# A list schedule's cost table in a hybrid decoder block: new estimates for scans, matmuls, transposes and GpSimd operations

## The chip, the core and the metric

The kernel runs on one core of a Trainium2 chip, as one launch. The metric is the device time of that launch in microseconds (us). The profile names the engines PE (TensorE matmul), PEld (TensorE's weight loads), DVE (VectorE), ACT (ScalarE), POOL (GpSimd) and SP (SyncE, which issues most DMAs). Each engine works off its own instructions in the order in which the program issued them, and waits on semaphores for the others.

## The reference, cut to what matters

```python
xn   = rms_norm(x, norm1_g)                         # x: 1024 tokens x 1024
proj = xn @ w_in                                    # to 44 blocks of 128 columns
q_sb, k_sb, v_sb, q_hg, f_hg, i_hg, g_hg, gate_sb, gate_hg = split_cols(proj, IN_SIZES)
# 8 stick-breaking heads of 64: z = q.k/8 under the strict causal mask
#   w = exp(log_sigmoid(z) - sum of softplus(z) over the keys between), o = w @ v
o_sb = stick_breaking_attention(rms_norm(q), rms_norm(k), v)
# 4 gated recurrent heads of 128: S_t = diag(f_t) S_{t-1} + (1-f_t) i_t^T, o_t = S_t^T q_t
o_hg = hgrn2_mixer(q_hg, f_hg, i_hg, g_hg, lb, hg_norm_g)
mixed = sigmoid(gate_sb) * (o_sb @ w_branch[:512]) + sigmoid(gate_hg) * (o_hg @ w_branch[512:])
h = x + mixed @ w_out
out = h + (silu(hn @ w_gate) * (hn @ w_up)) @ w_down     # hn = rms_norm(h, norm2_g)
```

All data are float32. The sums over keys in the attention and over time in the recurrent heads are running sums, which VectorE computes with its scan instruction.

## The kernel before, in words

Activations are kept transposed, channels on the 128 partitions and tokens along the free axis, in two halves of 512 tokens. A float32 product is made of three matmuls: both operands are split into a high part (rounded to the type fp32r, which the matmul takes) and a low part (the rest), and high x high, high x low and low x high are added in PSUM.

The kernel has stages one behind the other. **Stage 1**, the only one that the change touches, holds the first norm, the input projection, the attention heads and the recurrent heads. Behind it come the branch product (lines 774 to 810), the output product, the gated FFN and the down product, whose order is written out in the program and stays as it is.

Stage 1 is not issued in the order in which it is written down. `Plan` (lines 74 to 197) records every instruction as an operation with an engine, an **estimated duration** in us, a rank, the operations that must come before it and the buffers it uses. `Plan.issue` then runs a list scheduler: it steps a clock, keeps for each engine the time at which it is free, and at each step gives a free engine the first operation in its list that is ready and whose buffers are to be had. The list is sorted by rank, then by `way`, the longest chain of estimated durations from the operation to the end. What it issues is the real instruction; what stays of the plan is only the **order** on each engine. A result travels for a fixed estimated time (`FROM` and `TO`: 0.14 us, 0.2 us out of TensorE, 0.35 us into it, 2.0 us out of a DMA).

The estimates come from small helpers:

- `A` (line 360) for ScalarE and `V` (line 364) for VectorE: a constant and the number of elements per partition at 1200 or 960 per us.
- `G` (line 368) for GpSimd: a number given at each call.
- `M` (line 371) for a group of matmuls: columns by 2400 per us and 0.003 us for each matmul; `T` (line 377) for transposes; `L` (line 382) for loads on SP's queue: 350 KB per us, at least 0.47 us.

On them stand the parts that the prediction speaks of:

- `take_x` (line 441) loads x, splits it, and adds up the eight squared tiles, some on GpSimd, some on VectorE; `M(2048 * 2, ...)` in line 468 sums them over the channels, and `rstd` makes the norm's factor. Nothing that leaves a projection can go on before that factor.
- `proj` (line 474) issues one projected block of 128 channels and 512 tokens as 8 operations of 3 matmuls into one of three PSUM banks `pj`. Its rank is -1, so it is **filler**: TensorE takes it when nothing else is ready. The blocks come in one fixed order (`fill`, from the strings in line 30). A block for head pair u+1 has to wait until head pair u has released its buffers (`gate`, line 760); the 16 blocks "G" (the output gates) have no such wait. The last five blocks are "G".
- `split_w` (line 430) splits half a weight tile: the high part on GpSimd (`pool_copy`), the low part `ol` on VectorE.
- `scores` (line 548): six copies by DMA gather one attention head (`qs`, `ks`), then for each block of queries the matmuls `z` (two PSUM banks), on ScalarE the steps to softplus, on VectorE one add (`aa<-z,aa`), the **scan** (line 580) and the difference `ww<-z,aa` (line 584), which is the last reader of the bank `z`.
- `values` (line 589): transposes of the weights (`ms<-ident,ww`), the split into `th` and `tl`, and the product with v.
- `hgrn` (line 637): four scans of 128 tokens (line 649), seven levels of decayed products (line 657, `ms<-ql,dl`), the state update, and the sums by `sums` (line 489), whose high part is made on GpSimd.

Of the kernel before, what the change touches and what calls it, by code (L numbers as in the profile page):

```python
# [15 lines left out]
ALU = mybir.AluOpType  # L16
# [3 lines left out]
P = 128  # L20
# [180 lines left out]
def hybrid_block(ctx: ExitStack, tc, xT, wi, wb, wo, wg, wu, wd, vec, outT):  # L201
    nc = tc.nc
# [44 lines left out]
    ident = const1.tile([P, P], F32, name="ident")  # L247
# [10 lines left out]
    ones = const1.tile([P, P], F32, name="ones")  # L258
# [32 lines left out]
    def hs(h):  # L291
        return slice(h * HALF, (h + 1) * HALF)
# [42 lines left out]
    plan = Plan()  # L335
# [16 lines left out]
    def new(tag, shape=(P, HALF), dt=F32):  # L352
        pool, cap = where[tag]
        plan.ring(tag, cap)
        return Buf(tag, lambda: pool.tile(list(shape), dt, tag=tag, bufs=cap, name=tag))
# [6 lines left out]
        return plan.op("A", us, [(fn, args, kw)], rank, part=part, holds=holds)  # L362

    def V(fn, *args, n=HALF, aps=0, rank=0, part=False, holds=(), **kw):
        us = 0.07 + n / 960 + 0.061 * aps
        return plan.op("V", us, [(fn, args, kw)], rank, part=part, holds=holds)

    def G(fn, *args, us, rank=0, after=(), holds=(), **kw):
        return plan.op("G", us, [(fn, args, kw)], rank, after, holds=holds)

    def M(cols, mms, rank=0, after=(), holds=()):

        return plan.op("P", cols / 2400 + 0.003 * len(mms),
                       [(nc.tensor.matmul, m[:3], dict(start=m[3], stop=m[4])) for m in mms],
                       rank, after, holds=holds)

    def T(outs, after=(), holds=()):

        return plan.op("P", 0.11 * len(outs), [(nc.tensor.transpose, (o, i, ident), {})
                                               for o, i in outs], 0, after, holds=holds)  # L380

    def L(dst, src, kb, rank=0, after=(), part=False):
# [15 lines left out]
        A(act, a, a, AF.Exp)  # L398

    def pool_copy(dst, src, rank=0, after=(), holds=()):  # L400
        return G(nc.gpsimd.tensor_scalar, dst, src, 1.0, 0.0, op0=ALU.mult, op1=ALU.add, us=0.6,
                 rank=rank, after=after, holds=holds)

    lvl_mask = []
# [20 lines left out]
    last_load, last_split = [None], [None]  # L425

    def load(dst, src, kb):
        last_load[0] = L(dst, src, kb, rank=1, after=(last_load[0],))
# [12 lines left out]
    def take_x(h):  # L441
        ss, acc, ws, sqs = new("ms"), new("tail"), [[], []], []
        for k in range(KT):
            x = new("aa" if h == 0 else ("xf", "xq", "xi", "xg")[k // 2])
            load(x, xT[k][:, hs(h)], 256)
            if h == 0 and k in (0, 1, 3, 4):
                u, i = k % 3, k // 3
                n, v = fill[u]
                w = new("kb")
                load(w, wi[COL[n] + v][:, hs(i)], 256)  # L450
                ws[u].append(split_w(w))
            g = vt[:, V_N1 + k:V_N1 + k + 1]
            A(act, xh[k][h][:, hs(h)], x, AF.Copy, scale=g, aps=1, rank=2 - h)
            V(stt, xl[k][h][:, hs(h)], x, g, xh[k][h][:, hs(h)].bitcast(F32), op0=ALU.mult,
              op1=ALU.subtract, aps=1, rank=2 - h)
            if k == 0:
                A(act, acc, x, AF.Square, rank=1 - h)
            else:
                sq = new("ww")
                A(act, sq, x, AF.Square, rank=1 - h)  # L460
                sqs.append(sq)
        nv = 3 + h
        for sq in sqs[:7 - nv]:
            G(nc.gpsimd.tensor_tensor, acc, acc, sq, op=ALU.add, us=1.15, after=(last_split[0],))
        for sq in sqs[8 - nv:]:
            V(tt, sqs[7 - nv], sqs[7 - nv], sq, op=ALU.add, rank=1 - h)
        V(tt, acc, acc, sqs[7 - nv], op=ALU.add, rank=1 - h)
        M(2048 * 2, [(ss, ones, acc, True, True)])
        rstd(rr[h], ss, D, rank=1 - h)
        return ws  # L470

# [17 lines left out]
    def sums(out, src, w, n, after=()):  # L489

        hi, lo = new("th", dt=F32R)[:, :n], new("tl", dt=F32R)[:, :n]
        G(nc.gpsimd.tensor_scalar, hi, src, 1.0, 0.0, op0=ALU.mult, op1=ALU.add,
          us=0.05 + n / 930, holds=(lo,) if after else (lo, out))
        V(tt, lo, src, hi.bitcast(F32), op=ALU.subtract, n=n)
        return M(2 * n, [(out, w, hi, True, False), (out, w, lo, False, True)], after=after)

# [140 lines left out]
    def hgrn(hd, last):  # L637
        d = heads[hd]
        lbs, oml, nom = lb[:, hd:hd + 1], omlb[:, hd:hd + 1], nomlb[:, hd:hd + 1]
        state = None  # L640
        cs = [slice(c * P, (c + 1) * P) for c in range(4)]
        chunk = lambda t: t.rearrange("p (c t) -> p c t", t=P)
        for h in range(2):
            sf, q, vtok = d["hf", h], d["hq", h], d["hi", h]
            lf, key, bb, at = new("tmp"), new("kb"), new("kb"), new("kb")
            A(act, lf, sf, AF.Ln, bias=lbs, scale=oml, aps=2, holds=(key, bb, at))
            d["free hf", h] = V(ts, key, sf, nom, oml, op0=ALU.mult, op1=ALU.add, n=256, aps=2)
            for c in cs:
                V(nc.vector.tensor_tensor_scan, bb[:, c], lf[:, c], lf[:, c], 0.0, op0=ALU.add,
                  op1=ALU.min, n=P)  # L650
            pair = lambda t, m: t.rearrange("p (n u m) -> p n u m", u=2, m=m)
            G(nc.gpsimd.tensor_tensor, at, key, q, op=ALU.mult, us=1.15, after=(last,))
            dg = new("ms")
            last = sums(dg, at, ones_r, HALF, (last,))
            V(tt, chunk(at), chunk(dg),
              ident.rearrange("p (o t) -> p o t", o=1).to_broadcast([P, 4, P]), op=ALU.mult)
            for li, m in enumerate(LEVELS):
                nb = HALF // (2 * m)
                bv = pair(bb, m)
                if m == 1:  # L660
                    e1 = new("ql", (P, HALF // 2))
                    ev = e1.rearrange("p (n m) -> p n m", m=1)
                    V(tt, ev, bv[:, :, 1, :], bv[:, :, 0, :], op=ALU.subtract, n=256)
                    A(act, e1, e1, AF.Exp, n=256)
                    for t, u in ((key, 0), (q, 1)):
                        G(nc.gpsimd.tensor_tensor, ev, ev, pair(t, 1)[:, :, u, :], op=ALU.mult,
                          us=0.6)
                    lv = new("ms")
                    last = sums(lv[:, :256], e1, ones_r, 256, (last,))
                    V(nc.vector.copy_predicated, pair(at, 1)[:, :, 1, :],  # L670
                      lvl_mask[li - 1].rearrange("p c (n m) -> p (c n) m", m=1),
                      lv[:, :256].rearrange("p (n m) -> p n m", m=1), n=256)
                    continue
                rb = bv[:, :, 0, m - 1:m].to_broadcast([P, nb, m])
                dl, ql = new("dl"), new("ql", (P, HALF // 2))
                dv = pair(dl, m)
                V(tt, dv[:, :, 0, :], rb, bv[:, :, 0, :], op=ALU.subtract, n=256)
                V(tt, dv[:, :, 1, :], bv[:, :, 1, :], rb, op=ALU.subtract, n=256, part=True)
                A(act, dl, dl, AF.Exp)
                V(tt, ql.rearrange("p (n m) -> p n m", m=m), pair(q, m)[:, :, 1, :], dv[:, :, 1, :],  # L680
                  op=ALU.mult, n=256)
                V(tt, dv[:, :, 0, :], dv[:, :, 0, :], pair(key, m)[:, :, 0, :], op=ALU.mult, n=256)
                lv = new("ms")
                n = P - m
                last = M(8 * (n + 64), [(lv[:n, c * 64:(c + 1) * 64], dl[:, c * P:c * P + n],
                                         ql[:, c * 64:(c + 1) * 64], True, True)
                                        for c in range(4)], after=(last,))
                dst, src = pair(at, m)[:n, :, 1, :], lv[:n, :256].rearrange("p (n m) -> p n m", m=m)
                if m == 64:
                    V(nc.vector.tensor_copy, dst, src, n=256)  # L690
                else:
                    V(nc.vector.copy_predicated, dst,
                      lvl_mask[li - 1][:n].rearrange("p c (n m) -> p (c n) m", m=m), src, n=256)
            kd, ktok, qe, bl = new("tail"), new("tail"), new("tail"), new("bl", (P, 4))
            b3 = chunk(bb)
            V(tt, chunk(kd), b3[:, :, P - 1:P].to_broadcast([P, 4, P]), b3, op=ALU.subtract,
              holds=(ktok, qe, bl))
# [6 lines left out]
            d["free hq", h] = V(tt, qe, qe, q, op=ALU.mult)  # L704
            A(act, bl, b3[:, :, P - 1], AF.Exp, n=4)
            ds_ = new("ms")
            M(2048, [(ds_[:, c], ktok[:, c], vtok[:, c], True, True) for c in cs])
            before = []
            for i, c in enumerate(cs):
                before.append(state)  # L710
# [3 lines left out]
                else:  # L714
                    V(stt, st, state, bl[:, i:i + 1], ds_[:, c], op0=ALU.mult, op1=ALU.add, n=P,
                      aps=1)
                state = st
            op = new("ms")
            mms = []
# [2 lines left out]
                    mms.append((op[:, c], b, qe[:, c], True, False))  # L722
                mms.append((op[:, c], vtok[:, c], at[:, c], b is None, True))
            o, sq = new("tail"), new("tail")
            d["free hi", h] = M(4096, mms, holds=(o, sq))
            A(nc.scalar.copy, o, op, ps=True)
            A(act, sq, op, AF.Square, ps=True)
            ss = new("ms")
# [20 lines left out]
    for i, (nm, u) in enumerate(fill):  # L749
# [7 lines left out]
        elif i > 1:  # L757
            w = take_w(COL[nm] + u)
            for h in range(2):
                gate = None  # L760
                if nm != "G" and u:
                    d = heads[u - 1]
# [12 lines left out]
    for k in range(KT):  # L775
        t = mt.tile([P, S], F32, tag="ld", bufs=4, name="o32")
        nc.sync.dma_start(t, o_d[k])
        hi = op_.tile([P, S], F32R, name=f"oh{k}")
        lo = op_.tile([P, S], F32R, name=f"ol{k}")
# [7 lines left out]
    for i in range(KT):  # L787
# [11 lines left out]
        for h in range(2):  # L799
# [10 lines left out]
                                    op=ALU.subtract)  # L810
# [12 lines left out]
    with tc.tile_pool(name="wot", bufs=4, reuse_waits="tile") as ot_:  # L823
        seq = [0, 4, 1, 5, 2, 6, 3, 7]
        wq = [get_w(wo[seq.pop(0)])]
        for i in range(4):
# [14 lines left out]
            for e in range(2):  # L841
# [4 lines left out]
                for h in range(2):  # L846
# [8 lines left out]
                                            op0=ALU.mult)  # L855
# [3 lines left out]
                    else:  # L859
                        sq = tmp("sq")  # L860
# [67 lines left out]
    with ExitStack() as sta:  # L928
# [52 lines left out]
        for p in range(NP):  # L981
# [11 lines left out]
            c = fa.tile([P, 4, HALF], F32, tag="c", bufs=1, name="c")  # L993
# [33 lines left out]
    for o in DOWN:  # L1027
        first = o in (1, 6, 5)
        for p in range(NP):
# [16 lines left out]
            hi, lo = split(ra, wp, tags)  # L1046
# [73 lines left out]
```

## Time and profile before

| | before |
|---|---|
| median of 3 runs (lowest to highest) | 1580.96 us (1579.17 to 1581.63) |
| the profiled execution: its time, its span | 1582.63 us, 1580.9 us |
| TensorE's mean granted clock in it | 0.989 |
| last projection matmul of stage 1 starts at | 742.5 us |
| busy in the span: PE, PEld, DVE, ACT, POOL | 1531.5, 1249.6, 1223.1, 751.6, 215.3 us |

The profiled execution is one run, 1.67 us above the median; 1.7 us of its time lie around the span. In the lines of the profile L180 is the line in `Plan.issue` through which every instruction of stage 1 is issued, so a group of stage 1 is told apart by its tiles, written as out<-in. An engine's `q` (SPq) is its queue of semaphore and DMA instructions. A matmul's record overlaps the next one's, so that a busy PE is not yet a PE at its peak: the starts of two matmuls that follow each other are what shows its pace. The windows give the busy time of each engine in a stretch of the span, with the granted clock and what the DMA moved.

### The profile page before, as it was taken

To read this page: it belongs to the slowest core of one execution; us is meant where nothing else is said; L and a number is where in the kernel's file an instruction comes from. 1 tells how busy PE (TensorE), PEld (TensorE's weight loads), DVE (VectorE), ACT (ScalarE), POOL (GpSimd) and SP (SyncE) were. 2 spreads that over 40 slices of the span, in tenths; PEclk is the share of its full clock that TensorE was granted. 3 is DMA by queue.
4 is the path that set the end of the run, shared out by engine and by line. 5 is a ranking of instruction groups with operands and counts; after the bars stand their busy time and mean duration, and the time that the engine had idled before them with its cause. 6 is when DMAs were issued, how large, how long until landed. Compare 5 with 4: busy or idle time off the path is not lost.

```text
span 1580.9 us, 20533 instructions
## 1 busy us (share of the span) xinstructions
PE 1531.5 (97%) x7213; PEld 1249.6 (79%) x7213; DVE 1223.1 (77%) x2095; ACT 751.6 (48%) x1375; POOL 215.3 (14%) x231
## 2 busy tenths in 40 slices
PE   7999999999999999999999999999999999999999
PEld 5778887887778778888888878788888888778887
DVE  8798889999999776962657799888887777566553
ACT  5555767577657655452333363333333333244442
POOL 6121202301121000322441210000000000000000
PEclk9999999999999999999999999999999999999999
DMA  4303132113312232154334454666643333687672
GB/s 165 88 29 89 62 77 69 39 55 78 92 34 67 74 92 59 54 198 141 121 121 128 150 157 169 213 213 213 213 160 107 107 107 107 234 276 220 195 221 94
DMA packets 82247, 201.12 MB, mean 127 GB/s; under 512 B 9824, under 2 KB 11872, under 8 KB 80736
## 3 DMA queue, kind: packets, MB, share of 16 engines
q1 hardware_dynamic: 77536, 191.42, 38.5%
q10 hardware_dynamic: 4608, 8.39, 1.5%
q8 instruction: 57, 0.93, 0.3%
q14 instruction: 46, 0.38, 0.1%
HBM read 131.61 MB, written 55.57 MB: 118 GB/s over the span
## 4 chain that ended last, share of the span: by engine, by line
PE 71%; DVE 15%; DMA 5%; ACT 4%; issue 3%; SPq 1%; POOL 1%; DVEq 0%; ACTq 0%; POOLq 0%
PE f L908 25%; PE pj L180 16%; PE ms L180 6%; DVE aa L180 4%; PE f L1054 4%; PE f L1056 4%; PE f L1052 4%; PE pj L300 2%; PE pj L299 2%; PE pj L301 2%; DMA ks<-lk 2%; ACT aa L180 2%; PE z L180 2%; DMA rb<-act_d 1%; DVE ol L180 1%
## 5 line engine op out<-in xcount | busy, mean ns | idle before, releaser
L180 PE MATMUL pj<-ah,oh 128*128 128x512 f32 x704 | 288.9, 410 | 1.2 <-POOL oh L180 1.2
L180 PE MATMUL pj<-ah,ol 128*128 128x512 f32 x704 | 278.1, 395 | 0.4 <-DVE ol L180 0.4
L180 PE MATMUL pj<-al,oh 128*128 128x512 f32 x704 | 277.2, 394 | 0.0
L908 PE MATMUL f<-fh,oh 128*128 128x512 f32 x616 | 243.9, 396 | 3.2 <-ACT p L962 1.7
L908 PE MATMUL f<-fl,oh 128*128 128x512 f32 x616 | 243.5, 395 | 0.6 <-DVE fl L838 0.6
L908 PE MATMUL f<-fh,ol 128*128 128x512 f32 x616 | 243.2, 395 | 0.0
L235 ACT CAST oh<-w 128x512 fp32r<-128x512 f32 x168 | 102.4, 620 | 191.6 <-PE f L908 145.9
L180 PEld LDWEIGHTS pj<-ah,ol 128*128 128x128 f32 x704 | 133.5, 190 | 31.1 <-DVE ol L180 1.3
L180 PEld LDWEIGHTS pj<-ah,oh 128*128 128x128 f32 x704 | 134.3, 191 | 24.5 <-POOL oh L180 2.2
L180 PEld LDWEIGHTS pj<-al,oh 128*128 128x128 f32 x704 | 134.3, 191 | 22.3 <-issue 0.2
L236 DVE TENSOR_TENSOR ol<-w,oh 128x512 fp32r<-128x512 f32 x168 | 113.8, 684 | 37.7 <-ACT oh L235 37.4
L908 PEld LDWEIGHTS f<-fh,oh 128*128 128x128 f32 x616 | 115.5, 188 | 33.5 <-ACT p L962 2.2
L908 PEld LDWEIGHTS f<-fl,oh 128*128 128x128 f32 x616 | 115.5, 188 | 28.7 <-DVE fl L838 1.0
L908 PEld LDWEIGHTS f<-fh,ol 128*128 128x128 f32 x616 | 115.5, 188 | 28.1
L180 POOL TENSOR_SCALAR oh<-w 128x512 fp32r<-128x512 f32 x84 | 66.0, 787 | 396.2 <-PE pj L180 326.4
L1052 PE MATMUL f<-bh,ah 128*128 128x512 f32 x296 | 115.3, 393 | 4.0 <-ACT bh L235 4.0
L1054 PE MATMUL f<-bl,ah 128*128 128x512 f32 x296 | 117.5, 397 | 1.3 <-DVE bl L236 1.3
L1056 PE MATMUL f<-bh,al 128*128 128x512 f32 x296 | 117.3, 396 | 0.0
L236 DVE TENSOR_TENSOR al<-ra,ah 128x512 fp32r<-128x512 f32 x73 | 50.4, 690 | 73.1 <-ACT ah L235 72.9
L180 DVE TENSOR_TENSOR_SCAN aa<-aa 128x384 f32<-128x384 f32 (+3 forms) x96 | 95.1, 992 | 1.1
L235 ACT CAST ah<-ra 128x512 fp32r<-128x512 f32 x73 | 45.5, 623 | 102.8 <-PE f L1054 95.3
L180 DVE TENSOR_TENSOR ol<-w,oh 128x512 fp32r<-128x512 f32 x84 | 62.0, 739 | 18.7 <-POOL oh L180 18.1
(272 smaller groups left out, 3015.1 us busy)
## 6 DMA issues: line engine op xcount, KB each, us to landing
w<-wi SPq DMA_DIRECT2D x42, 512.0 KB, 3.6
rb<-act_d SPq DMA_DIRECT2D x73, 256.0 KB, 4.0
w<-wg SPq DMA_DIRECT2D x22, 512.0 KB, 3.8
w<-wu SPq DMA_DIRECT2D x22, 512.0 KB, 4.1
w<-wd SPq DMA_DIRECT2D x22, 512.0 KB, 6.7
wd_d<-ds SPq DMA_DIRECT2D x44, 256.0 KB, 5.2
act_d<-c SPq DMA_DIRECT2D x11, 1024.0 KB, 3.9
act_d<-bs SPq DMA_DIRECT2D x44, 256.0 KB, 3.3
```

Source lines behind the costliest of these rows:

```text
L180: fn(*[a.real() if isinstance(a, View) else a for a in args], **{k: v.real() if isinstance(v, View) else v for k, v in kw.items()})
L235: pin(nc.scalar.copy(hi, src))
L236: pin(nc.vector.tensor_tensor(lo, src, hi.bitcast(F32), op=ALU.subtract))
L299: nc.tensor.matmul(out, hi[:, ws], a[ka][0][:, hs(h)], start=first and i == 0, stop=False)
L300: nc.tensor.matmul(out, hi[:, ws], a[ka][1][:, hs(h)], start=False, stop=False)
L301: nc.tensor.matmul(out, lo[:, ws], a[ka][0][:, hs(h)], start=False, stop=last and i == n - 1)
L908: nc.tensor.matmul(out, a[i][:, ws], bl[k][j], start=start and k == 0 and i + j == 0, stop=k == 3 and i == 1, skip_group_check=True)
L1052: nc.tensor.matmul(bank[d], hi[:, ws], bh, start=first and p == 0, stop=False, skip_group_check=True)
L1054: nc.tensor.matmul(bank[d], hi[:, ws], bl, start=False, stop=False, skip_group_check=True)
L1056: nc.tensor.matmul(bank[d], lo[:, ws], bh, start=False, stop=p == NP - 1, skip_group_check=True)
```

## The change

Only estimated durations change. No instruction, buffer, rank or dependence is added or taken away, and the computed result is the same; the scheduler sees other numbers and may issue stage 1 in another order.

```diff
     def V(fn, *args, n=HALF, aps=0, rank=0, part=False, holds=(), **kw):
-        us = 0.07 + n / 960 + 0.061 * aps
+        cycles = 2 * n if fn == nc.vector.tensor_tensor_scan else n
+        us = 0.067 + cycles / 960 + 0.061 * aps
...
-    def M(cols, mms, rank=0, after=(), holds=()):
+    def M(cols, mms, rank=0, after=(), holds=(), us=None):
-        return plan.op("P", cols / 2400 + 0.003 * len(mms),
+        return plan.op("P", us or cols / 2255 + 0.003 * len(mms),
...
     def T(outs, after=(), holds=()):
-        return plan.op("P", 0.11 * len(outs), [(nc.tensor.transpose, (o, i, ident), {})
+        return plan.op("P", 0.11 * len(outs) - 0.08, [(nc.tensor.transpose, (o, i, ident), {})
...
     def pool_copy(dst, src, rank=0, after=(), holds=()):
-        ... us=0.6,
+        ... us=0.68,
...
         for sq in sqs[:7 - nv]:                       # take_x
-            G(nc.gpsimd.tensor_tensor, acc, acc, sq, op=ALU.add, us=1.15, after=(last_split[0],))
+            G(nc.gpsimd.tensor_tensor, acc, acc, sq, op=ALU.add, us=1.5, after=(last_split[0],))
-        M(2048 * 2, [(ss, ones, acc, True, True)])
+        M(2048, [(ss, ones, acc, True, True)])
...
         G(nc.gpsimd.tensor_scalar, hi, src, 1.0, 0.0, op0=ALU.mult, op1=ALU.add,      # sums
-          us=0.05 + n / 930, holds=(lo,) if after else (lo, out))
+          us=0.07 + n / 840, holds=(lo,) if after else (lo, out))
...
-            G(nc.gpsimd.tensor_tensor, at, key, q, op=ALU.mult, us=1.15, after=(last,))   # hgrn
+            G(nc.gpsimd.tensor_tensor, at, key, q, op=ALU.mult, us=1.3, after=(last,))
...
                         G(nc.gpsimd.tensor_tensor, ev, ev, pair(t, 1)[:, :, u, :], op=ALU.mult,
-                          us=0.6)
+                          us=1.0)
...
-                last = M(8 * (n + 64), [...], after=(last,))           # a level, n = 128 - m
+                last = M(0, [...], after=(last,), us=0.43 + 0.003 * n)
...
-            M(2048, [(ds_[:, c], ktok[:, c], vtok[:, c], True, True) for c in cs])
+            M(0, [(ds_[:, c], ktok[:, c], vtok[:, c], True, True) for c in cs], us=0.86)
...
-            d["free hi", h] = M(4096, mms, holds=(o, sq))
+            d["free hi", h] = M(0, mms, holds=(o, sq), us=0.215 * len(mms))
```

ScalarE's estimates, the loads' and the travel times stay as they are.

More of the change, by code (lines that the diff above doesn't have):

```diff
@@ L400, in pool_copy @@
     def pool_copy(dst, src, rank=0, after=(), holds=()):
-        return G(nc.gpsimd.tensor_scalar, dst, src, 1.0, 0.0, op0=ALU.mult, op1=ALU.add, us=0.6,
+        return G(nc.gpsimd.tensor_scalar, dst, src, 1.0, 0.0, op0=ALU.mult, op1=ALU.add, us=0.68,
                  rank=rank, after=after, holds=holds)
@@ L684, in hgrn @@
                 n = P - m
-                last = M(8 * (n + 64), [(lv[:n, c * 64:(c + 1) * 64], dl[:, c * P:c * P + n],
+                last = M(0, [(lv[:n, c * 64:(c + 1) * 64], dl[:, c * P:c * P + n],
                                          ql[:, c * 64:(c + 1) * 64], True, True)
-                                        for c in range(4)], after=(last,))
+                                        for c in range(4)], after=(last,),
+                         us=0.43 + 0.003 * n)
                 dst, src = pair(at, m)[:n, :, 1, :], lv[:n, :256].rearrange("p (n m) -> p n m", m=m)
```

## The prediction

> **What bounds the kernel now.** I read the windows along stage 1 first, to see which engine sets its pace and its end, then the chain of waits for its last part.
>
> ```profile
> 240.00:280.00 40.00, 37.17 (x186) 29.86 (x185) 38.96 (x72) 27.53 (x54) 8.79 (x11) 1.00 0.31 71
> ...
> 680.00:700.00 20.00, 20.00 (x107) 17.12 (x106) 11.20 (x20) 10.39 (x16) 3.10 (x5) 1.00 0.48 161
> 700.00:720.00 20.00, 20.00 (x90) 16.57 (x89) 11.65 (x10) 10.51 (x12) 11.42 (x8) 1.00 0.86 312
> 720.00:740.00 20.00, 20.00 (x90) 16.58 (x89) 3.08 (x4) 5.97 (x9) 3.75 (x5) 1.00 0.35 119
> 740.00:760.00 20.00, 20.00 (x87) 16.14 (x87) 9.17 (x14) 5.26 (x8) 4.43 (x3) 1.00 0.40 132
> ```
>
> ```profile
> 692.59 50.35 PE pj L180 x222
> ```
>
> The columns of a window are its length and the busy time of PE, PEld, DVE, ACT and POOL, then the granted clock. Two things are to be seen. In the middle of the stage VectorE is as full as TensorE (38.96 of 40 us). But the stage ends with 50.35 us of nothing but projection matmuls, 222 of the 240 that the last five filler blocks "G" hold, with VectorE mostly free, and TensorE goes into the next stage without a gap (20.00 of 20 us from 740). So the attention and the recurrent heads are done about 50 us before the stage is. **The stage lasts as long as TensorE's work and TensorE's waits.** The work is the same in any order. What a new order can change is the sum of the waits, and each microsecond of wait that goes takes a microsecond off the filler at the end, which has 50 to give.
>
> So I looked at the waits of TensorE's weight loads, from 60 us to the end of the stage, and for the time before 60 us (the second fence, its largest row).
>
> ```profile
> PEld z L180 <- DVE ww L180: 15.6, 32, 1.2
> PEld z L180 <- issue: 6.9, 3, 2.5
> PEld ms L180 <- DVE tl L180: 6.6, 12, 1.6
> PEld ms L180 <- issue: 6.4, 11, 1.7
> PEld z L180 <- DMA ks<-lk: 3.9, 2, 2.5
> PEld ms L180 <- DVE kb L180: 2.9, 5, 0.9
> PEld z L180 <- DVE tl L180: 1.4, 1, 1.4
> PEld ms L180 <- ACT dl L180: 1.2, 1, 1.2
> PEld ms L180 <- PE pj L180: 1.0, 1, 1.0
> PEld ms L180 <- ACT tail L180: 1.0, 1, 1.0
> ```
>
> ```profile
> PEld ms L180 <- DVE tail L180: 7.2, 2, 3.9
> ```
>
> The columns are the sum, the count and the longest. A weight load normally runs ahead of its matmul, so its wait overstates what TensorE loses:
>
> ```profile
> 91.47 0.39 PE L180 MATMUL pj<-ah,ol 128*128 128x512 f32 x1
> 92.66 0.73 PE L180 MATMUL z<-ks,qs 128*128 128x512 f32 x2 [0.80 <-DVE ww L180]
> ```
>
> Here, at the longest wait of the first row (1.2 us), the next matmul starts 1.19 us after the one before, where the pace of the filler is 50.35/222 = 0.227 us. TensorE lost 0.96 us; 0.25 us of the wait was cover. Taking 0.25 off each wait, three classes stand after 60 us: **z waiting for its bank** (DVE ww), 15.6 - 32 x 0.25 = 7.6 us; **z waiting for the gathered heads** (the five of "issue" and DMA, which I read as one kind because they are as long as one another), 10.8 - 5 x 0.25 = 9.6 us; **the seven other rows**, 20.5 - 32 x 0.25 = 12.5 us. Before 60 us the two waits for the sum of squares cost 7.2 - 0.5 = 6.7 us. All of it, 36 us, is the ceiling of what an order can bring, and most of it has causes that the edit does not price.
>
> **The change part by part.** *The scans.* This is the edit with the largest error behind it.
>
> ```profile
> L180 DVE TENSOR_TENSOR_SCAN aa<-aa 128x512 f32<-128x512 f32 x48 | 61.8, 1289 | 0.5
> ...
> L180 DVE TENSOR_TENSOR ww<-z,aa 128x512 f32<-128x512 f32 x48 | 32.6, 680 | 1.1 <-PE ms L180 0.9
> L180 DVE TENSOR_TENSOR tl<-ms,th 128x512 fp32r<-128x512 f32 x48 | 32.4, 679 | 10.5 <-ACT th L180 10.4
> ...
> L180 DVE TENSOR_TENSOR_SCAN aa<-aa 128x384 f32<-128x384 f32 x16 | 15.8, 986 | 0.2
> L180 DVE TENSOR_TENSOR_SCAN kb<-tmp 128x128 f32<-128x128 f32 x32 | 15.2, 486 | 0.3 <-ACT tmp L180 0.3
> ...
> L180 DVE TENSOR_TENSOR tl<-aa,th 128x512 fp32r<-128x512 f32 x16 | 12.5, 788 | 0.8 <-POOL th L180 0.7
> ```
>
> A scan of 512 took 1289 ns beside 680 ns for a difference of 512. The old estimate was the same for both, 0.07 + 512/960 = 0.60 us; the new one is 0.067 + 1024/960 = 1.13 us, so the plan now sees 0.53 us more at each large scan, and over the stage (48 x 512 + 16 x (384 + 256 + 128) + 32 x 128)/960 = 42.7 us more work on VectorE. The difference ww, which frees the bank z, stands right behind the scan. The old plan therefore put a z up to 0.53 us too early on TensorE's queue, in front of filler that could have run; the waits behind ww cost 7.6/32 = 0.24 us each, less than that error. With the right price a block of three filler matmuls (0.68 us) goes ahead of such a z. I take 5 of the 7.6 us; the bounds are 7.6 and 0.
>
> *The same error in the other rows.* tl, kb and dl come late because VectorE's queue is longer than planned; the scans in front of them are one part of that. Another part the edit leaves: tl takes 788 ns when both its operands lie in SBUF and GpSimd has just made one of them, and 679 ns when one lies in PSUM. I take a third of 12.5 us, 4 us. Bounds: 8 us (two thirds), and 4 us the wrong way, since a new order can make new waits of the same sort.
>
> *Start.* The adds of the squares on GpSimd go from 1.15 to 1.5 us:
>
> ```profile
> L180 POOL TENSOR_TENSOR tail<-tail,ww 128x512 f32<-128x512 f32 x7 | 11.6, 1661 | 3.1 <-ACT ww L180 3.1
> ```
>
> They took 1.66 us. Four stand ahead of the first sum and three of the second, so the plan sees these 1.4 and 1.05 us later and can put two and one blocks of 0.68 us ahead, where blocks are ready: 2.0 us. I take 1.5; bounds 2.5 and 0.
>
> *Matmuls.* Three filler matmuls are priced 1536/2255 + 0.009 = 0.690 us instead of 0.649; the trace has 3 x 0.227 = 0.680. Over the stage the plan's TensorE gets 704 x 0.041 = 29 us longer. That is right as a price and has a bad side: filler priced too low gave each wait some 5% more real cover than planned, and for waits that the plan still sees too short this cover goes. The clearest are the gathered heads:
>
> ```profile
> ks<-lk SPq DMA_DIRECT2D x16, 256.0 KB, 5.0
> ```
>
> Planned, the six copies take 6 x 256/350 + 2.0 = 6.4 us to the last landing; the last two alone need 5.0 us each from issue to landing. In 6.4 planned us the old plan puts 6.4 x 0.041/0.690 = 0.38 us more filler than the new one. For eight heads that is 3.0 us. I take 2 us of loss, since two of the eight do not wait today; bounds 0 and 6.5 us, the upper one with two more of these:
>
> ```profile
> 131.70:135.10 3.40, 3.40 (x9) 2.72 (x10) 1.89 (x5) 0.99 (x3) 0.00 (x0) 0.50 0.02 6
> ...
> 133.33 0.63 PE L180 MATMUL pj<-ah,oh 128*128 128x512 f32 x1
> 133.76 0.63 PE L180 MATMUL pj<-al,oh 128*128 128x512 f32 x1
> ```
>
> (a window and, below it, the timeline.) After such a wait the granted clock was 0.50 for 3.4 us and filler started every 0.43 us instead of 0.227, which costs 3.4 x (1 - 0.227/0.43) = 1.6 us beyond the wait; none of these waits was over 2.5 us. The Trainium skill, "TensorE: Matmul & The Clock Gate", section "What's actually happening", gives the half clock to an array that was idle for at least one window of about 3.4 us; by that sentence a somewhat longer load wait would cost only itself, and the sum of bounds here would be 3.0 us. The trace decides against that reading: a shorter wait was enough.
>
> *The rest* (transposes, the levels, the state products, GpSimd's copies and products) moves prices by tenths of a microsecond for operations off the end; I give them nothing of their own, and the 4 us the wrong way cover them. The stage behind has its loads under the 50 us of filler, and 8 us less leave 42.
>
> Sum: -5 - 4 - 1.5 + 2 = **-8.5 us**. On the profiled execution that is 1582.6 - 8.5 = 1574.1; it was 1.7 us above the median of the runs, so for the median 1581.0 - 8.5 = **1572.5**. The bounds add up to -7.6 - 8 - 2.5 = -18 and 0 + 4 + 0 + 6.5 = +10.5 us.
>
> **The rivals.** *Nothing measurable.* TensorE and VectorE both get longer in the plan, by 29 us of filler and 42.7 us of scans, in a stage of 743 us; where both stretch alike, the order hardly moves, and what is left late are operations whose length no constant holds. For it speaks the pair of 788 and 679 ns; against it, that 32 of the waits stand behind the one difference that follows a scan. The waits then shift by no more than 3 us: 1578 to 1584. The Trainium skill, "SBUF — State Buffer", section "SBUF: two separate sides", says that a VectorE operation with two SBUF inputs and a GpSimd operation that reads SBUF lock each other out for a whole instruction. The pair of rows agrees, with 109 ns on the mean; if this lock stands behind most waits, this rival is the outcome.
>
> *Slower, by lost cover.* The dearer filler takes away cover at every wait that the plan prices too short, not only at the loads: 3.0 us at the heads, two more half-clock stretches 3.2 us, and at the 32 other waits, with an estimated 1.5 us between cause and use, 6% of that each, 2.9 us; together 9.1 us. With z's 5 us taken off, 4.1 us remain: 1585; without them 1590. It decides where z gains less than 9 us and the other rows nothing. For it speaks that five waits of the heads are already the longest ones; against it, that scans make VectorE's planned lateness larger than filler's.
>
> *Slower by an accident of order.* A list schedule can get worse with better prices: `way` grows for the attention chain and recurrent work is put behind it. It would take 50 us at the end to show there, so it can only make waits in the middle, some 5 us: 1586.
>
> **How the numbers follow.** About 0.2% (3.2 us) is what a measurement of this kernel can tell from no change. Forecast 0.52; nothing measurable 0.22; lost cover 0.16; accident of order 0.10. The last two make 0.26 for slower. The range reaches from 1563 (the best bound, 1581 - 18) to 1588, which takes in both slower cases but for their worst; it leaves out about 2 in 10. The forecast's own range is 1563 to 1577.8.
>
> **What would show it.** Right: the row of z behind ww falls from 15.6 to under 7 us; the 50.35 us of filler at the end get shorter by about the gain; as many projection matmuls, of the same pace, start in all. The wait for the tail falls from 7.2 to about 5.5 us; the waits for the gathered heads stay at or above 10.8 us with the half-clock stretches beside them. Wrong: the row behind ww stays; or it falls and the rows of tl, issue and ks grow by as much; or the stage's end is no longer filler, in which case TensorE's waits do not set it.

## The result, and the profile after

The changed kernel is **slower**: 1601.55 us (median of 4 runs, 1601.33 to 1610.1) beside 1580.07 us before, 21.5 us more. The ratio is 1.0149 with a 95% interval of 1.0128 to 1.0171; it is one of means, which the run of 1610.1 us pulls up, and the medians alone give 1.0136. The profiled execution took 1610.1 us with a span of 1608.4 us; it is the longest of the four, 8.5 us above the median, so its waits are read for their places and kinds, and the medians for sizes.

Stage 1 ends later, and still with filler. The last part of the chain of waits, after:

```profile
713.22 57.83 PE pj L180 x255
```

It ends at 771.0 us where the stage before ended at 692.59 + 50.35 = 742.9, 28.1 us later; the whole span grew by 27.5. So all of the loss is in stage 1. There are 255 filler matmuls at the end instead of 222: filler was not used up in the middle, though TensorE waited more there. The windows show where; the same 37 us in both traces, projection matmuls alone (the count in brackets behind PE's busy time). Before:

```profile
272.60:309.50 36.90, 26.76 (x106) 18.93 (x106) 3.37 (x5) 0.00 (x0) 1.00 0.11 31
```

After:

```profile
232.00:272.60 40.60, 33.20 (x137) 24.82 (x135) 3.74 (x6) 0.00 (x0) 1.00 0.13 39
272.60:309.50 36.90, 0.39 (x2) 0.10 (x1) 0.68 (x1) 0.00 (x0) 0.65 0.12 29
309.50:350.00 40.50, 28.62 (x107) 19.60 (x108) 2.75 (x4) 0.00 (x0) 0.98 0.25 61
```

In 36.9 us the new order issues no filler at all (the two are the tail of the last matmuls); the old one issued 106 - 2 = 104 more, 104 x 0.227 = 23.6 us of work that now lies at the end. The granted clock fell to 0.65 in the hole. TensorE's timeline, after, at its edges and inside:

```profile
272.59 0.40 PE L180 MATMUL pj<-ah,ol 128*128 128x512 f32 x1
274.25 0.86 PE L180 MATMUL ms<-ql,dl 128*96 128x64 f32 x8 [1.26 <-ACT dl L180]
280.10 1.73 PE L180 MATMUL ms<-ql,dl 128*112 128x64 f32 x8 [4.99 <-DVE kb L180]
...
302.77 0.55 PE L180 MATMUL ms<-ident,ww 128*128 128x128 f32 x3
305.31 1.22 PE L180 MATMUL z<-ks,qs 128*128 128x512 f32 x2 [1.99 <-DVE ww L180]
...
309.51 0.73 PE L180 MATMUL pj<-ah,oh 128*128 128x512 f32 x1
...
314.64 0.22 PE L180 MATMUL z<-ks,qs 128*128 128x128 f32 x1
```

The block that ends at 272.6 is hg1, the sixteenth of the fixed order; the one that starts at 309.5 is q2. Its gate is the last gather of q for the fourth attention head (`d["free q"]`, lines 554 and 763 of the kernel before), and that gather needs `qs`, which the third head holds until its last z, at 305.31. The fourth head's first z is at 314.64; before, it was at 270.5. Between 272 and 303 TensorE works mostly on the recurrent head (`ms<-ql,dl`) and waits for VectorE, and no new z is started. VectorE's timeline, after, shows how:

```profile
268.17 1.12 DVE L180 TENSOR_TENSOR ww<-z,aa 128x512 f32<-128x512 f32 x2
...
274.02 1.27 DVE L180 TENSOR_TENSOR_SCAN aa<-aa 128x512 f32<-128x512 f32 x1
...
278.07 1.21 DVE L180 TENSOR_TENSOR_SCAN aa<-aa 128x512 f32<-128x512 f32 x1
...
304.57 0.68 DVE L180 TENSOR_TENSOR ww<-z,aa 128x512 f32<-128x512 f32 x1
```

The two scans are done by 279.3, and the difference behind them comes at 304.57, 25 us later, right behind the transposes at 302.77 that read `ww` tiles. From the order I read that the seven `ww` tiles were full, since the transposes of the weights had been put behind the recurrent head's levels. The counts in the trace agree: by 272 us the third head had written nine `ww` tiles (33 writes in all, 12 for each head), and three of its transposes had run (75 in all, 36 for each head), which set two tiles free. Nine less two are the seven there are. No run below changes these tiles by themselves.

The waits of TensorE's weight loads, after, from 60 us to the end of the stage:

```profile
PEld z L180 <- issue: 17.1, 10, 3.2
PEld ms L180 <- issue: 12.2, 15, 5.1
PEld z L180 <- DVE ww L180: 9.5, 17, 2.2
```

z behind ww fell from 15.6 to 9.5 us, as forecast in kind. The waits for the gathered heads went up, which TensorE's own rows name as what they are. Before, from 60 to 743 us:

```profile
PE z L180 <- DMA ks<-lk: 12.2, 6, 2.4
```

After, from 60 to 770 us:

```profile
PE z L180 <- DMA ks<-lk: 14.7, 7, 3.1
PE z L180 <- DMA ks<-hk: 3.3, 5, 1.0
```

### The profile page after: what moved, and what is told of

Read it like the earlier page. It is cut to its first block, busy times and chain, and to the rows that moved or that the text cites. A ratio compares the mean times of both kernels' runs of the same rounds, so it can differ in the third digit from the quotient of the medians.

```text
span 1608.4 us, 20518 instructions
## 1 busy us (share of the span) xinstructions
PE 1545.6 (96%) x7213; PEld 1262.3 (78%) x7213; DVE 1230.1 (76%) x2095; ACT 754.4 (47%) x1375; POOL 213.3 (13%) x231
## 4 chain that ended last, share of the span: by engine, by line
PE 69%; DVE 14%; DMA 6%; issue 4%; ACT 3%; SPq 2%; POOL 1%; DVEq 0%; ACTq 0%; POOLq 0%
PE f L910 22%; PE pj L180 17%; PE ms L180 7%; PE f L1056 4%; PE f L1058 4%; PE f L1054 4%; DMA ks<-lk 3%; PE pj L299 2%; PE pj L300 2%; PE pj L301 2%; DVE aa L180 2%; PE z L180 2%; SPq L180 2%; DVE dl L180 1%; DVE kb L180 1%
## 5 line engine op out<-in xcount | busy, mean ns | idle before, releaser
L236 DVE TENSOR_TENSOR ol<-w,oh 128x512 fp32r<-128x512 f32 x168 | 113.8, 684 | 39.3 <-ACT oh L235 39.2
L180 PE MATMUL z<-ks,qs 128*128 128x128 f32 (+3 forms) x192 | 53.9, 370 | 25.3 <-DMA ks<-lk 17.1
```

Of the source, the lines that this page charges most:

```text
L180: fn(*[a.real() if isinstance(a, View) else a for a in args], **{k: v.real() if isinstance(v, View) else v for k, v in kw.items()})
L236: pin(nc.vector.tensor_tensor(lo, src, hi.bitcast(F32), op=ALU.subtract))
```

## The experiments

Two theories stood after the result. **Gated filler**: the new order makes the third attention head late, and the filler, being in a fixed order, has to stand still at q2. **Lost cover**: the dearer matmul column takes filler from in front of every wait that the plan sees too short. The rival to both was that VectorE had become the bound. Each time below is the median with its ratio to the kernel before on the same chip.

### The scan's price alone

```diff
-        us = 0.07 + n / 960 + 0.061 * aps
+        cycles = 2 * n if fn == nc.vector.tensor_tensor_scan else n
+        us = 0.067 + cycles / 960 + 0.061 * aps
```

> The kernel before, with the scan's price alone changed (the line in V). Theory, the gated filler: the dearer scan reorders the third and fourth attention head, the block q2 has to wait for the fourth head's gathers, and TensorE has no filler for some 20 to 40 us. Then this edit alone brings most of the loss: 1592 to 1605 us, with a hole of over 15 us between the last matmul of hg1 and the first of q2. Rival, lost cover (TensorE's and GpSimd's prices): this edit alone gives 1570 to 1580, with fewer waits of z behind ww.

1588.22 us, ratio 1.0060 (1.0039 to 1.0081): less than the theory's 1592, more than the rival's 1580. The projection matmuls in the windows:

```profile
272.60:309.50 36.90, 8.50 (x34) 6.07 (x34) 2.06 (x3) 0.00 (x0) 0.72 0.27 59
```

and the weight loads' waits:

```profile
PEld z L180 <- DVE ww L180: 5.6, 7, 2.4
```

Both mechanisms are in this one run. The waits of z behind ww fell from 15.6 us (32) to 5.6 us (7), and hg1's last matmul starts at 269.0 us, 7.6 us ahead of the kernel before (276.6). Then q2 has to wait, until 296.7. The 7.6 us are the filler's place and not all a gain: by 269 us this run had started 767 projection matmuls where the kernel before had started 747, but 66 of z for 72. Twenty matmuls of filler at 0.227 us less six of z at about the same are an estimated 3 us. So the row gained what was forecast, the time some 3 us up to the hole, and the whole run lost 8.5 us.

### All new prices but the scan's

The change with the V line as before.

> The changed kernel with the scan's old price (all other new prices stay). Theory, the gated filler: no hole at q2, 1575 to 1586 us. Rival, lost cover by dearer filler: 1585 to 1600, with longer waits of z behind the gathered heads and behind ww, spread over the stage.

1600.34 us, ratio 1.0126 (1.0094 to 1.0159). The theory's half was right (no hole: hg1's last matmul at 288.5, q2's first at 288.7), its time was wrong, and the rival's nearly right, 0.3 us over its upper end: the stage's last projection matmul starts at 762.9 us, 20.4 us later than before, with no hole over 6 us in its filler. When it reached q2 its filler was 11.9 us late; the rest came after, spread over many waits.

```profile
PEld z L180 <- DVE ww L180: 25.5, 43, 1.8
PEld ms L180 <- DVE tl L180: 11.2, 17, 1.3
```

So the new prices hold two losses, and the 21.5 us are not one of them alone.

### Three ungated blocks ahead of the gate, with the new prices and with the old

```diff
-FILL = ["GgGaifq", "gaGfiqGG", "gaGGGiqGfGG", "gGGGGG"]
+FILL = ["GgGaifq", "gGGGafiq", "gaGGGiqGfGG", "gGGGGG"]
```

> The changed kernel with three ungated G blocks moved in the filler's order, from behind the unit-2 blocks to ahead of q2. Theory, the gated filler: the three blocks (3 x 48 x 0.227 = 33 us of matmuls) fill the hole, the end of stage 1 comes 20 to 28 us sooner, 1570 to 1582 us. If the new prices also do what the prediction said, it is 1572 or less. Rival, VectorE itself is the bound in the new order (the recurrent heads hold up the attention): the hole fills, but filler was not what was missing and the end stays, 1595 to 1603.

> The kernel before with the same three G blocks moved ahead of q2: what the filler's order does without the new prices. Theory: the kernel before has almost no hole at q2 (hg1 ends at 276.6, q2 starts at 277.5 us), so there is little to fill, 1574 to 1584 us. Rival, the filler's order is worth 20 us by itself whatever the prices: 1555 to 1565.

With the new prices 1585.82 us, ratio 1.0037 (1.0024 to 1.0051), 15.7 us less than the change; with the old prices 1583.51, ratio 1.0021 (1.0003 to 1.0038), 3.8 us more than the kernel before beside it. The first, in the window of the hole:

```profile
272.60:309.50 36.90, 24.50 (x94) 17.06 (x95) 0.67 (x1) 2.32 (x4) 0.99 0.38 98
```

The hole is full (94 matmuls for 2), the stage's last filler starts at 749.8 instead of 770.7, and since the same move gains nothing with the old prices, what it gave back is the hole. VectorE as the bound is out. The time is 3.8 us above the upper end of what was expected: what is left, 6.2 us over the kernel before, I put down to the other loss; no run takes it apart.

### The column's price alone, and all the others without it and the scan's

```diff
-        return plan.op("P", cols / 2400 + 0.003 * len(mms),
+        return plan.op("P", cols / 2255 + 0.003 * len(mms),
```

> The kernel before with the price of a column of matmul alone changed (2400 to 2255 per us), the scan left cheap. Theory, lost cover: this one price makes most of the 20 us that all prices but the scan's cost: 1590 to 1602 us, no hole at q2, longer waits of z behind ww than the 15.6 us of before. Rival: the loss comes from the other prices (levels, transposes, GpSimd), and this alone gives 1577 to 1585.

> The changed kernel with the old price of the scan and the old price of a matmul column; the new prices of levels, transposes, state products and GpSimd stay. Theory, lost cover by the filler's price: 1576 to 1586 us. Rival, the small prices reorder the stage: 1590 or more.

The column alone: 1610.42 us, ratio 1.0201 (1.0182 to 1.0220), the largest loss of the prices that were run alone, above what was expected. The others without column and scan: 1593.45, ratio 1.0089 (1.0074 to 1.0104). That is in the rival's range: the small prices of levels, transposes, state products and GpSimd, which had been given nothing of their own, reorder the stage and cost 13.4 us by themselves. z behind ww, in the first and in the second:

```profile
PEld z L180 <- DVE ww L180: 25.0, 42, 1.9
```

```profile
PEld z L180 <- DVE ww L180: 11.9, 24, 1.1
```

With the two runs above this makes a table of that one wait: column old and scan old 15.6 (before) and 11.9; column new and scan old 25.0 and 25.5; column old and scan new 5.6; both new, in the change, 9.5. So far dearer filler goes with a longer wait and dearer scans with a shorter one; a later pair of runs, below, goes the other way for the filler. It is some 10 us of the 30, though; the others are spread over rows that also grew (ks<-lk 12.0, tl 8.9).

### The scan's price with the gates covered

The scan's line as above and `FILL = ["GgGaifq", "gGGGafiq", "gGaGGiqGfGG", "gGGGGG"]`: three G blocks ahead of q2, one ahead of q3.

> The kernel before with the scan's new price, and the ungated G blocks moved: three ahead of q2 and one ahead of q3. Theory: the gain of the right scan price shows once the hole at the gate is filled; before the hole this order was 7.6 us ahead of the kernel before, so 1568 to 1576 us, no hole over 3 us. Rival: filling the hole gives back what the alone scan price lost and no more, 1577 to 1585.

1580.35 us, ratio 0.9994 (0.9978 to 1.0010): the rival's number. z behind ww was 5.1 us and the hole at q2 gone, but the waits for the gathered heads grew:

```profile
PEld z L180 <- issue: 22.0, 11, 3.0
```

That is twice the 10.8 us of before, and pointed to a price which the change had left alone, the DMA's. In the profiled run the stage's last projection matmul started at 738.7 us, 3.8 us ahead of the kernel before, and what lies behind it took 842.9 us of the span where it took 838.4 before. So part of a small gain may have been lost behind stage 1; of the 16 traces none has less than 833.6 us there or more than these 842.9, and differences of a few microseconds can't be put down to stage 1 alone.

### The travel time of a DMA's result

```diff
-    FROM = {"P": 0.2, "D": 2.0}
+    FROM = {"P": 0.2, "D": 4.0}
```

> The changed kernel with the G blocks moved as in the run beside it, and the plan's travel time of a DMA's result set from 2.0 to 4.0 us, nearer to the 5.0 us from issue to landing. Theory: the waits of z for the gathered heads, some 20 us with filler ahead of q2, are a price that is too low, and fall below 8 us; half-clock stretches go with them: 1568 to 1578. Rival: the later gathers only make the attention later and new holes at the gates: 1585 or more.

> The kernel before with one change: a DMA's result travels 4.0 us in the plan instead of 2.0. Theory, the waits for the gathered heads are a price that is too low whatever the rest: they fall from 10.8 us to under 4 and four half-clock stretches go, 1564 to 1574 us. Rival: the gain of 1.1% needed the other new prices, 1577 or more.

> The changed kernel, filler in its old order, with the travel time of 4.0 us. Theory A, the hole at q2 is one outcome of a schedule on the edge, and a plan that shifts the gathers gets another one: the hole may close, 1560 to 1575. Theory B, the hole comes from the scan's price and the gate as such, and stays without the G blocks ahead: 1585 to 1600.

On the change with the G blocks of the run above: 1560.78 us, ratio 0.9887 (0.9868 to 0.9906), under the theory's range. On the change as it is, with this line alone: 1560.09, ratio 0.9883 (0.9860 to 0.9907), 41.5 us less than the change. On the kernel before: 1584.55, ratio 1.0036 (1.0025 to 1.0047), a loss, in the rival's range. TensorE's rows of the second:

```profile
PE z L180 <- DMA ks<-lk: 3.8, 4, 2.0
...
PE z L180 <- DVE ww L180: 1.1, 3, 0.6
```

and its filler in the window of the hole, without any G block moved:

```profile
272.60:309.50 36.90, 24.32 (x96) 17.50 (x96) 2.79 (x4) 0.00 (x0) 1.00 0.13 37
```

Theory A for that run was right: another plan, no hole. That this plan had none is luck as far as the runs show. On the kernel before the waits for the heads fell as well (ks<-lk 3.5 us), and yet it lost: a hole opened at another gate, inside the block hi2, and the weight loads' rows of z behind ww (18.8 us) and ms behind tl (10.0 us) grew too. Its projection matmuls in the hole:

```profile
366.90:397.00 30.10, 0.43 (x3) 0.15 (x1) 0.68 (x1) 0.00 (x0) 0.67 0.18 40
```

### Taking the column's price back in the best order

The kernel of 1560.78 us with 2400 instead of 2255, and the same with the filler in its old order:

> The kernel of 1560.8 us (all new prices, G blocks ahead, travel time 4.0) with the old price of a matmul column, 2400 per us. Theory, filler priced too low is cover for waits that the plan does not see: the waits of z behind ww fall from 9.7 to about 5 us, 1550 to 1558 us. Rival: with everything else priced right, the right price of a column is the best one, 1563 to 1580.

> The kernel of 1548.6 us (all new prices but the matmul column's, travel time of a DMA 4.0) with the filler's blocks in their old order, no G ahead of q2 and q3. Theory, gated filler: one or two holes of over 10 us come back at q2 or q3, 1562 to 1585 us. Rival: with these prices the order of the filler does not matter, 1545 to 1553.

The first is the fastest of the study, **1548.55 us, ratio 0.9803 (0.9778 to 0.9828)**, under its range. The second took 1570.49, ratio 0.9943 (0.9926 to 0.9960), inside its range. z behind ww in the first, and in the kernel of 1560.78 us that it came from:

```profile
PEld z L180 <- DVE ww L180: 3.5, 4, 2.0
```

```profile
PEld z L180 <- DVE ww L180: 9.7, 16, 3.0
```

A price known to be 5% too low is worth 12 us here. With the old order of the filler two holes are back, at q2 and at q3 (projection matmuls, second kernel):

```profile
254.80:274.40 19.60, 0.27 (x2) 0.09 (x1) 1.27 (x2) 0.00 (x0) 0.56 0.27 64
442.60:460.20 17.60, 0.24 (x2) 0.09 (x1) 0.68 (x1) 0.00 (x0) 0.81 0.24 67
```

37.2 us of holes, 22 us of time: the gate matters in a second order too.

The second kernel has a partner: it differs from the change with the travel time of 4.0 us (1560.09 us, above) by the column's price alone. Here the old, too low price is the slower one, by 10.4 us (ratios 0.9943 and 0.9883), and z waits longer behind ww with it. The second kernel, then its partner with the new price:

```profile
PEld z L180 <- DVE ww L180: 12.2, 8, 4.3
```

```profile
PEld z L180 <- DVE ww L180: 5.0, 13, 1.0
```

So the column's new price cost 30 and 12 us in two pairs of runs and some 7 us, hardly clear of the noise, in a third; it brought 10 us in the fourth, where the old one opened the two holes. What it does to the time hangs on the order it meets.

### Attention ahead of the recurrent heads; longer travel into TensorE

The change with the matmuls and the ScalarE and VectorE operations of `scores` at rank 0.5 (its gathers stay as they are); and the column's price alone with

```diff
-    TO = {"P": 0.35}
+    TO = {"P": 0.6}
```

> The changed kernel with the operations of scores ranked ahead of the other stage work (rank 0.5), so that the recurrent heads cannot hold up the third attention head before its gathers. Theory, the order between attention and recurrent head made the hole: it shrinks from 37 us to under 20, 1584 to 1594 us. Rival: the hole has another cause and stays, or the recurrent heads are held up instead, 1600 or more.

> The kernel before with the right price of a matmul column alone (as in the run of 1610.4 us), and with the plan's travel time of a result into TensorE raised from 0.35 to 0.6 us. Theory, lost cover: the dear filler cost 30 us because results reach TensorE later than planned; a longer planned travel gives cover back without touching a price, and the waits of z behind ww fall from 25.0 to under 15 us: 1580 to 1597 us. Rival, the price merely led to a bad order by accident: no better than chance, 1603 or more, or the waits of z stay.

With attention first 1595.58 us, ratio 1.0110 (1.0088 to 1.0132), just above its range; the hole at q2 shrank from 36.9 to 15.1 us (279.6 to 294.7). So the order between attention and recurrent head has a part in the hole, and ranking one ahead is not enough to close it. With longer travel 1602.26, ratio 1.0134 (1.0104 to 1.0163), 8 us less than the column alone, outside the lost-cover range; and the wait that should have fallen below 15 us did not, which is the second half of the rival:

```profile
PEld z L180 <- DVE ww L180: 28.9, 41, 1.6
```

So a longer travel does not stand in for cheap filler. Filler priced too low went with shorter waits of z in three pairs and with longer ones in the fourth, so lost cover is an argument with support and not shown; why the right price alone costs 30 us and not 10 stays open. The rival that any new order is partly an accident was not tested as such, by many small changes of no meaning. The signs speak for it: the column's price and the travel time of 4.0 us each gained in one order and lost in another. What is shown is the hole at the gate, by the trace and by filling it.

## Why the prediction was wrong

- *The stage lasts as long as TensorE's work and TensorE's waits.* Right: the stage ends with filler in all 16 traces, and the span follows its end to within about 5 us.
- *Each microsecond of wait that goes takes a microsecond off the filler at the end, which has 50 to give.* This is the main step that failed, and with it the price of the rival that came true, the accident of order ("It would take 50 us at the end to show there, so it can only make waits in the middle, some 5 us"). Filler is not on hand at any time: it comes in one order, and its next block waited for an attention head. The hole was 36.9 us, and filling it gave back 15.7 of the 21.5. The gate stands in `gate` and in the plan's `after`, and I had described it; I did not ask what the new order does to the operation that opens it.
- *The scan's price*, -5 us. Right for its row: with it alone z lost 5.6 - 7 x 0.25 = 3.9 us instead of 7.6. The time never showed it: alone the price cost 8.5 us, and with the gates covered the ratio was 0.9994.
- *The same error in the other rows*, -4 us. In kind right for tl, 6.6 to 2.6 us after; but ms behind "issue" doubled, 6.4 to 12.2 us, with 5.1 of it one wait in the hole.
- *Start*, -1.5 us. Right in kind: the wait for the tail fell from 7.2 to 3.3 us. That is one wait of the two, and other waits before 60 us grew: behind tl from 1.3 to 2.3 us, behind al from none to 2.4.
- *Matmuls*, +2 us, with 6.5 as the upper bound (its own parts, 3.0 and two times 1.6, make 6.2). Mis-sized, and not of one size: alone +30 us, 12 us in the best order, and 10 us the other way in one more. I bounded it by the eight gathers and the half-clock stretches, as if a new price could only touch waits that the trace already showed. The row of z behind ww went from 15.6 (32 waits) to 25.0 us (42), so there were waits that had not been there.
- *The rest*, nothing of its own. This failed too: the levels, transposes, state products and GpSimd's prices together (the adds of the squares among them), without scan and column, cost 13.4 us. I put them at nothing because they are tenths of a microsecond on operations off the end; by the same gates and ranks they move the order all the same, by more than the 4 us the wrong way that were to cover them. Which of them does it stays open.
- *Slower, by lost cover*, 1585 to 1590: right in the sign of the outcome, at a fifth to two fifths of its size. As a mechanism it has three pairs of runs for it and one against.
- *What would show it*: the row behind ww "under 7 us" came to 9.5; the filler at the end got longer, 57.83 us, where the forecast wanted it shorter. One sign of being wrong came as written: ww's row fell by 6.1 us and the two rows of issue grew by 16.0 together, z's from 6.9 to 17.1 us and ms's from 6.4 to 12.2.
- The half clock: the hole's granted clock of 0.65 fits the rows on which the bound was built. The sentence of the Trainium skill ("TensorE: Matmul & The Clock Gate", "What's actually happening"), idle for a window of about 3.4 us, does not fit even the 4.99 us wait in the hole: the wait began at 275.1 us, and the granted clock was 0.50 from 277.0 to 297.5 us, so from 1.9 us into it. The trace decides against the sentence as it stands. Shorter waits, of 1.7 to 3.1 us, have their half-clock stretches too.

## What to carry to other kernels

In a list schedule that only sets the order, a price is a lever on what stands in front of what; making some prices right and leaving others can cost more than it brings, here 30 us for one right price. Before changing prices, follow the filler: list what each block waits for, and ask what happens to the operation that opens the next gate; a few ungated blocks kept ahead of a gate insure against a hole. Then try the price behind the waits that the trace shows, and measure: one line, the DMA's 2.0 us set to 4.0, turned a loss of 21 us into a gain of 18 on the changed kernel, and lost 6 us on the kernel before. A price's effect in one order is not its effect in the next, so a table of prices is judged as a whole.

## What the runs showed of the hardware

In these traces the granted clock fell where TensorE waited. With the gathers priced at 4.0 us on the change it was 0.993 over the whole profiled execution, in the change 0.978, in the kernel before 0.989. It is not only the gathers: on the kernel before with 4.0 us their waits fell too, and the clock was 0.987, with 0.67 in the hole inside hi2.
